# Gating and splitting gelu values inside their PSUM banks, a gates' grid in runs of 16 frames, and one-hot rows by one pointer instruction a frame, in a streaming encoder step

## The chip, the cores and the metric

One core of a Trainium2 chip runs the whole step as one program. The metric is the device time of an execution in microseconds; the kernel before was run three times. TensorE multiplies matrices (its weight loads are shown as a row of their own, PEld), VectorE (DVE) and ScalarE (ACT) work element by element and can read and write PSUM, GpSimd (POOL) works element by element in SBUF and issues the indirect gathers, SyncE (SP) issues the other DMAs. Each engine runs its queue in order.

## The reference

The step is one layer over 1024 prompt frames and 32 sample frames of width 1024: input projection, differential attention, a gated recurrence, output projections, and then PEER, a retrieval over 16384 single-neuron experts. The change touches PEER alone. For each frame, 8 heads each pick 16 experts by the best sums of two key halves; an expert's number is 128 i + j.

```python
s = jnp.einsum('thcd,hckd->thck', q, sub_keys.astype(jnp.float32))
sv, si = lax.top_k(s, P_TOPK)
comb = (sv[:, :, 0, :, None] + sv[:, :, 1, None, :]).reshape(P_TBLOCK, P_HEADS, P_TOPK * P_TOPK)
cv, ci = lax.top_k(comb, P_TOPK)
...
gate = jax.nn.softmax(cv, axis=-1)
hid = jax.nn.gelu(jnp.einsum('thkd,td->thk', down[e], xs).astype(jnp.float32), approximate=False)
return jnp.einsum('thk,thkd->td', (gate * hid).astype(xs.dtype), up[e])
```

The output is the residual sum, normed. Everything is float32; the large products are made of operands split into a rounded high part and a low part, three products for one.

## The kernel before, in words

Frames come in tiles of 128 (0 to 7) and a tile "S" of 32 sample frames. Tiles 0 to 4 ("dense", 640 frames) go through all 16384 experts; tiles 5, 6, 7 and S gather the rows of their own experts. Generators yield pieces of work, each with the time it is taken to cost, and a loop weaves them into one program: `gemm` (the projections, then the dense experts), `attn`, `routing` (the best 16, `topk`), `scatter` (the gates of the dense tiles), `rows` (the gathered experts). `PACED` holds the rows and the routing on VectorE behind what `gemm` has asked of it. A planner then orders each engine's queue by a model of instruction times.

**The gates' grid** (`scatter` and `grid`, L1084 to L1148, 739 to 1604 us). For each dense frame the 128 gates are placed into a 128 x 128 grid by a product of one-hot matrices: rows `am` (is this the expert's i), columns `bm` (is this its j, times the gate). Four frames make a step, 160 steps in all. `bm` is one comparison of 512 elements on VectorE against broadcast operands (L1126) and one multiplication by the gates on GpSimd (L1139). `am` is in every other step one such comparison on VectorE, in the others five ScalarE instructions (L1134, L1135). Four 128 x 128 products go into one bank, and ScalarE copies it (L1091) into the staging tile `stg`. After 16 frames `stg` goes to DRAM, 1 MB, as `W_d`, in which the 8 columns of a group lie side by side for each frame.

**The dense experts** (`hidden` L1156, `stage_v` L1198). A column e stands for the 128 experts 128 i + e. `hidden(e)`: two loads of weights, split by ScalarE and GpSimd (L254, L255, tiles `dh`, `dl`), 24 products into each of two PSUM banks of 320 frames, then ScalarE's gelu from the bank into an SBUF tile `vg` (L1174; the first six columns before `stage_v`, four of them into a tile `early`). `gated(e)`: every 8 columns the gates are loaded from `W_d`, two tiles of 1.25 MB; two VectorE multiplications by the gates, of 320 elements each, whose gates lie 8 elements apart (L1214); then `split`: a rounding copy on ScalarE (L254) and the rest by a subtraction on VectorE (L255), both over 640 elements, into `vwh` and `vwl`. Each four columns are multiplied by the up weights `uh`, `ul`: 8 blocks of two banks of 12 products, each bank added to the sums `acc` in SBUF by VectorE (L1279). All these banks come in turn from one pool of five; a further bank `ws` serves the sum of the sample's runs, and two hold the gathered rows' sums `xp`.

**The gathered rows** (L1044 to L1050, L1031). For each of 416 rows: an indirect gather issued by GpSimd, a product and sum over 1024 elements on VectorE (L1047), gelu and gate on ScalarE, and a multiplication and addition into `xp` in PSUM on VectorE (L1031).

The two lines of the split:

```python
A.activation(h, src, AF.Copy)
(lo_engine or G).tensor_tensor(out=l, in0=src, in1=h.bitcast(F32), op=OP.subtract)
```

Of the kernel before, what the change touches and what calls it, by code (L numbers as in the profile page):

```python
# [7 lines left out]
F32 = mybir.dt.float32  # L8
# [17 lines left out]
JB = 8  # L26

# tiles of frames that share a pass over w_in; tiles that share one over the other weights
AG = [[0, 1, 2, 3, 4], [5, 6, 7, "S"]]
CDG = [[0, 1, 2], [3, 4], [5, 6, 7, "S"]]  # L30
# tiles whose expert products run over all experts; the other ones gather the rows of theirs
# [3 lines left out]
# tiles whose scores wait in DRAM, and how many heads are routed at a time if not all  # L35
DEFER = [6, 7]
HG = {5: 2, 6: 4}
# places of weights in the rings, as they come and in two parts: output stages, then projections
RINGS = [(4, 4), (2, 3), (3, 4), (4, 4)]
SCS = [2, 2, 4, 3]  # L40
# places of the recurrence's tiles, by group
DEEP = [(2, 10), (1, 5)]
# frames on their way into the projections, by group
PRE = [2, 1]
# places of: gathered rows; expert weights, as they come and split; best halves; one-hots
RB, VR, VB, BB, OHB = 4, 3, 2, 4, 4
# engines that make the one-hot rows, in turn
AMS = "DA"
# of the splits of weights in the output stages, one in so many goes to the vector engine
CSH = 2  # L50
# banks of the large products: so many of so many in turn from the extra pool of that size
GX = (3, 6, 3)
# columns of experts whose hidden values wait in the place of the sums
GB, GE = 2, 6
# the time that a gathered row and a one-hot half step are taken to cost
GC, SC = 1.65, 1.0
# which streams keep behind the large products in which phase, and by how much less
# [10 lines left out]
def step_kernel(ctx, tc, x_prompt, x_sample, cache_kT, cache_v, state, norm1, w_in, lam_params,  # L68
# [21 lines left out]
    def bank_of(name):  # L90
        return lambda: P[name].tile([128, 512], F32, name=name, tag=name)
# [4 lines left out]
    gb_bank, gv_bank = bank_of("gb"), bank_of("gv")  # L96
    TURN = [0]

    def gm_bank():
        """ the banks of the large products; more of them while the attention asks for none """  # L100
        TURN[0] += 1
        key = "gx" if "gx" in P and TURN[0] % GX[1] < GX[0] else "gm"
        return P[key].tile([128, 512], F32, name="gm", tag="gm")
# [7 lines left out]
    # ---------------------------------------------------------------- constants  # L111
# [27 lines left out]
    def masks(ct):  # L139
        """ what the attention and the recurrence need of constants """  # L140
        # masks of [s, t]: s <= t inside a block of 16; a block of 16 against the one before it in 32
# [8 lines left out]
        # s - 16*(t//16) in 0..15 and s <= t  # L150
# [5 lines left out]
        # s - 32*(t//32) in 0..15, t in the second half of its 32  # L156
# [4 lines left out]
        # resets of the running sums at each block of 16  # L161
# [9 lines left out]
        # the weight of the second map  # L171
# [10 lines left out]
        # lower bounds of the gates, columns: heads  # L182
# [13 lines left out]
    # ---------------------------------------------------------------- scratch in DRAM  # L196
# [26 lines left out]
    def span(ts):  # L223
        """ runs of consecutive token columns: (first column here, first column in DRAM, width) """
# [10 lines left out]
    def rstd_of(pool, ss, n, width, T=128, tag=""):  # L235
        """ (ss/width + eps)^-0.5 for a [T, n] tile of sums of squares """
        ms = pool.tile([128, n], F32, name="ms" + tag, tag="ms" + tag)
        V.tensor_scalar(ms[:T], ss[:T], 1.0 / width, 1e-6, op0=OP.mult, op1=OP.add)
        # a first guess from the exponent's bits, then Newton's steps
# [17 lines left out]
    def mm3(out, pairs):  # L257
        """ sum of products of operands split into two parts each """
# [6 lines left out]
    def transposed_half(bank, xs, T, hi, lo, off):  # L265
        """ four blocks of 128 columns into a pair of tiles """
# [17 lines left out]
    def load_split(pool, src, tag, rbufs, bufs, nk=KD, share=0):  # L284
        """ a block of weights [128, nk, 256], in two parts, by four blocks of 128 rows """
# [12 lines left out]
    # ---------------------------------------------------------------- input projection  # L298
    BDONE, READY, DONE = set(), set(), set()
    BEST = {}  # L300
    # 0: up to the products over all experts, 1: their start, 2: their steady state
    PHASE = [0]

    def natural(g, b, i, ws, wk):
        """ a block of the projection of one tile, frames by rows """
# [1147 lines left out]
```

## Time and profile before

| | |
|---|---|
| median of 3 runs | 3572.49 us (3570.26 to 3582.99) |
| profiled execution: span | 3583.5 us |
| TensorE, VectorE | 3257.4 us (91%), 3063.6 us (85%) |
| GpSimd, ScalarE | 2074.9 us (58%), 1454.3 us (41%) |

The profile is of one execution. Its own time is given only as the span from the first to the last instruction; that span is 11.0 us above the median of the runs, and no time around it is listed. The busy shares are means over stages with different limits, so the stages are read one by one in the section on rows. Times in the rows are microseconds, "mean ns" is nanoseconds. A name behind "<-" after a bar is what the engine last waited for.

### The profile page before, as it was taken

The numbers are of one execution on the slowest core, as the hardware profiler recorded it, in microseconds if no ns is written. First come the engines' busy times: TensorE is split into PE (matmuls) and PEld (weight loads), VectorE is DVE, ScalarE is ACT, GpSimd is POOL, SyncE is SP. The second block draws the span as 40 slices with busy tenths as digits, with TensorE's granted clock in tenths as the row PEclk, the third lists the DMA queues.
The fourth block names the chain that finished last, engine by engine and source line by source line (L and its number), as shares of the span: only waits on it lengthen the run. The fifth ranks groups of instructions, "written<-read, shape, count | busy, mean of one in ns | idle before, by whom it ended". The sixth has DMA issues, their size and how long they took to land.

```text
span 3583.5 us, 59911 instructions
## 1 busy us (share of the span) xinstructions
PE 3257.4 (91%) x21639; PEld 3128.0 (87%) x21639; DVE 3063.6 (85%) x6101; ACT 1454.3 (41%) x3508; POOL 2074.9 (58%) x1339
## 2 busy tenths in 40 slices
PE   7999899989998887868989988899999999999995
PEld 7989899867877886767889888899999999999994
DVE  3354468999787999999999999988989989989998
ACT  3544334445665544543333323333333333333332
POOL 2322125546444556666666577777767666776674
PEclk9999999999998998978999999999999999999997
DMA  4554364454465644478788777799888998998987
GB/s 164 166 158 149 107 215 158 152 151 152 148 217 183 206 130 150 152 249 298 258 289 296 275 271 290 266 341 351 316 315 335 337 343 296 346 338 333 336 325 265
DMA packets 357304, 880.58 MB, mean 246 GB/s; under 512 B 30960, under 2 KB 190192, under 8 KB 299664
## 3 DMA queue, kind: packets, MB, share of 16 engines
q1 hardware_dynamic: 297104, 440.52, 36.8%
q0 software_dynamic: 59904, 436.23, 33.0%
q8 instruction: 171, 2.80, 0.3%
q14 instruction: 125, 1.02, 0.1%
HBM read 784.47 MB, written 92.14 MB: 245 GB/s over the span
## 4 chain that ended last, share of the span: by engine, by line
PE 28%; DVE 19%; issue 2%; DMA 2%; POOL 2%; ACT 0%; POOLq 0%; ACTq 0%; DVEq 0%
PE gv L263 9%; PE gv L262 9%; PE gv L261 9%; DVE row L1047 5%; DVE xp L1031 5%; DVE vg L1214 2%; DVE acc L1279 2%; DMA ur<-in_p_up_dram 2%; DVE vwl L255 2%; POOL row L1044 1%; DVE oh L967 1%; POOL dl L255 1%; DVE ef L972 1%; POOL ul L255 0%; DVE si L902 0%
## 5 line engine op out<-in xcount | busy, mean ns | idle before, releaser
L1044 POOL DMA_INDIRECT row<-in_p_rows_dram,ei x384 | 559.8, 1458 | 340.2 <-DVE xp L1031 172.2
L255 POOL TENSOR_TENSOR wl<-wr,wh 128x1024 fp32r<-128x1024 f32 x160 | 397.3, 2494 | 532.2 <-ACT wh L254 483.0
L261 PE MATMUL gv<-vxh,dh 128*128 128x320 f32 x2048 | 646.5, 316 | 42.4 <-DVE acc L1279 23.6
L263 PE MATMUL gv<-vxh,dl 128*128 128x320 f32 x2048 | 644.8, 316 | 34.8 <-POOL dl L255 34.7
L261 PE MATMUL gv<-vwh,uh 128*128 128x320 f32 x2048 | 636.2, 311 | 14.1 <-ACT uh L254 8.3
L262 PE MATMUL gv<-vwl,uh 128*128 128x320 f32 x2048 | 636.8, 311 | 12.4 <-DVE vwl L255 12.3
L262 PE MATMUL gv<-vxl,dh 128*128 128x320 f32 x2048 | 642.3, 314 | 0.0
L263 PE MATMUL gv<-vwh,ul 128*128 128x320 f32 x2048 | 633.9, 310 | 1.1 <-POOL ul L255 1.0
L1047 DVE CUSTOM_DVE_ANT_0 row<-row,xg 128x1024 f32<-128x1024 f32 x416 | 627.0, 1507 | 3.1 <-DMA sc<-scs 2.3
L1031 DVE SCALAR_TENSOR_TENSOR xp<-row,hid,xp 128x1024 f32<-128x1024 f32 x412 | 527.8, 1281 | 78.2 <-ACT hid L1050 78.0
L1049 ACT ACTIVATE hid<-hid 128x1 f32<-128x1 f32 x416 | 84.0, 202 | 936.1 <-DVE hid L1047 926.3
L255 POOL TENSOR_TENSOR ul<-ur,uh 128x512 fp32r<-128x512 f32 x256 | 359.7, 1407 | 135.2 <-ACT uh L254 125.6
L261 PEld LDWEIGHTS gv<-vxh,dh 128*128 128x128 f32 x2048 | 393.5, 192 | 50.1 <-DVE acc L1279 27.3
L263 PEld LDWEIGHTS gv<-vxh,dl 128*128 128x128 f32 x2048 | 392.7, 192 | 43.1 <-POOL dl L255 42.0
L255 POOL TENSOR_TENSOR dl<-dr,dh 128x512 fp32r<-128x512 f32 x256 | 365.1, 1433 | 82.0 <-ACT dh L254 73.9
L261 PEld LDWEIGHTS gv<-vwh,uh 128*128 128x128 f32 x2048 | 386.7, 189 | 17.1 <-ACT uh L254 9.3
L262 PEld LDWEIGHTS gv<-vwl,uh 128*128 128x128 f32 x2048 | 386.9, 189 | 16.5 <-DVE vwl L255 16.5
L262 PEld LDWEIGHTS gv<-vxl,dh 128*128 128x128 f32 x2048 | 393.9, 192 | 0.0
L263 PEld LDWEIGHTS gv<-vwh,ul 128*128 128x128 f32 x2048 | 386.3, 189 | 2.7 <-POOL ul L255 2.5
L1139 POOL TENSOR_TENSOR ohB<-ohB,tr 128x512 f32<-128x512 f32 x160 | 195.0, 1224 | 264.3 <-DVE ohB L1126 201.5
L1214 DVE TENSOR_TENSOR vg<-vg,gw 128x320 f32<-128x320 f32 x248 | 253.4, 1022 | 27.7 <-ACT vg L1174 17.5
L261 PE MATMUL gm<-xh,wh 128*128 128x320 f32 (+1 forms) x768 | 254.0, 331 | 0.0
(328 smaller groups left out, 7490.5 us busy)
## 6 DMA issues: line engine op xcount, KB each, us to landing
dr<-in_p_downT_dram SPq DMA_DIRECT2D x256, 256.0 KB
ur<-in_p_up_dram SPq DMA_DIRECT2D x256, 256.0 KB
wr<-in_w_in_dram SPq DMA_DIRECT2D x88, 512.0 KB
W_d<-stg SPq DMA_DIRECT2D x40, 1024.0 KB
gw<-W_d SPq DMA_DIRECT2D x32, 1280.0 KB
wr<-in_p_wq_dram SPq DMA_DIRECT2D x48, 512.0 KB
wr<-in_w_out_dram SPq DMA_DIRECT2D x24, 512.0 KB
wr<-in_w_a_dram SPq DMA_DIRECT2D x12, 512.0 KB
```

What stands on the lines that cost most here:

```text
L255: (lo_engine or G).tensor_tensor(out=l, in0=src, in1=h.bitcast(F32), op=OP.subtract)
L261: PE.matmul(out, lh, rh, start=(i == 0), stop=False)
L262: PE.matmul(out, lh, rl, start=False, stop=False)
L263: PE.matmul(out, ll, rh, start=False, stop=(i == n - 1))
L967: V.tensor_tensor(out=oh[:T], in0=cf[:T, h].unsqueeze(2).to_broadcast([T, 16, NCAND]), in1=iota_c[:T].unsqueeze(1).to_broadcast([T, 16, NC ...
L1031: V.scalar_tensor_tensor(out=acc, in0=row[:, D:], scalar=hid[:, k:k + 1], in1=acc if k else first, op0=OP.mult, op1=OP.add)
L1044: G.indirect_dma_start(out=row, out_offset=None, in_=p_rows, in_offset=bass.IndirectOffsetOnAxis(ap=ei[:, k:k + 1], axis=0))
L1047: V.tensor_tensor_reduce(out=row[:, 0:D], in0=row[:, 0:D], in1=xt, scale=1.0, scalar=0.0, op0=OP.mult, op1=OP.add, accum_out=h)
L1049: A.activation(h, h, AF.Gelu)
L1139: G.tensor_tensor(out=bm, in0=bm, op=OP.mult, in1=tr[:, 2, xs].unsqueeze(2).to_broadcast([128, 4, 128]))
L1214: V.tensor_mul(gh, gh, G_[h][:, :, j])
L1279: V.tensor_add(acc[:, db, cs], acc[:, db, cs], ps[:, :CHUNK])
```

## The change

The gelu of all columns after the first six stays in its PSUM bank. Gating and split work bank by bank, 320 frames at a time, with the bank as operand; the tile `vg` goes away, and the first six columns all use `early`. Every sixth bank asked for once the dense stage has begun is the spare bank `ws`. The grid in DRAM now holds, for each group of 8 columns, runs of 16 frames for one column; the staging copy writes that order. The one-hot rows are made frame by frame, 128 elements at a time, by VectorE comparisons against a number per partition, for `bm` with the gate as a second such number in the same instruction; GpSimd's multiplication goes away. The sample's sum takes its banks from the large pool. Only comments differ elsewhere.

```diff
-GB, GE = 2, 6
...
+GE = 6
...
-    gb_bank, gv_bank = bank_of("gb"), bank_of("gv")
+    gb_bank = bank_of("gb")
     TURN = [0]
 
+    def gv_bank():
+
+        TURN[0] += 1
+        pool, tag = (wsp, "ws") if PHASE[0] and TURN[0] % 6 == 0 else (P["gv"], "gv")
+        return pool.tile([128, 512], F32, name="gv", tag=tag)
...
-                    ps = ws_bank()
+                    ps = gv_bank()
...
-    W_d = dram([128 // JB, 128, NV, JB], "W_d")
     SB = 16
+    W_d = dram([128 // JB, 128, NV // SB, JB, SB], "W_d")
...
-        A.activation(stg[:, :, q:q + 4, :].rearrange("p b t j -> p t b j"),
-                     ps.rearrange("p (t b j) -> p t b j", t=4, j=JB), AF.Copy)
+        A.activation(stg[:, :, :, q:q + 4],
+                     ps.rearrange("p (t b j) -> p b j t", t=4, j=JB), AF.Copy)
         if q + 4 == SB:
-            o = 128 * DENSE.index(t) + s0
-            SP.dma_start(out=W_d[:, :, o:o + SB, :].rearrange("b i t j -> i b t j"), in_=stg)
+            o = (128 * DENSE.index(t) + s0) // SB
+            SP.dma_start(out=W_d[:, :, o].rearrange("b i j t -> i b j t"), in_=stg)
...
-                stg = sct.tile([128, 128 // JB, SB, JB], F32, name="stg", tag="stg", bufs=1)
+                stg = sct.tile([128, 128 // JB, JB, SB], F32, name="stg", tag="stg", bufs=1)
...
-                    xs = slice(s0 + q, s0 + q + 4)
-
-                    def equal(out, row):
-                        V.tensor_tensor(out=out, in0=iota_r.unsqueeze(1).to_broadcast([128, 4, 128]),
-                                        in1=tr[:, row, xs].unsqueeze(2).to_broadcast([128, 4, 128]),
-                                        op=OP.is_equal)
-
+                    for u in range(4):
+                        c = s0 + q + u
+                        if AMS[(s0 + q) // 4 % len(AMS)] == "A":
+
+                            A.activation(am[:, u], iota_r, AF.Abs, bias=tr[:, 3, c:c + 1])
+                        else:
+                            V.tensor_scalar(am[:, u], iota_r, tr[:, 0, c:c + 1], None, op0=OP.is_equal)
+                        V.tensor_scalar(bm[:, u], iota_r, tr[:, 1, c:c + 1], tr[:, 2, c:c + 1],
+                                        op0=OP.is_equal, op1=OP.mult)
                     if AMS[(s0 + q) // 4 % len(AMS)] == "A":
...
-                        for u in range(4):
-                            c = s0 + q + u
-                            A.activation(am[:, u], iota_r, AF.Abs, bias=tr[:, 3, c:c + 1])
                         A.activation(am, am, AF.Relu, bias=1.0, scale=-1.0)
-                    else:
-                        equal(am, 0)
-                    equal(bm, 1)
-                    G.tensor_tensor(out=bm, in0=bm, op=OP.mult,
-                                    in1=tr[:, 2, xs].unsqueeze(2).to_broadcast([128, 4, 128]))
...
-        if GB <= e < GE:
-            g = VX["early"][:, e - GB]
-        else:
-            g = wk.tile([128, NV], F32, name="vg", tag="vg", bufs=GB)
+        VX[e] = []
         for cs in CS:
             ps = gv_bank()
             mm3(ps[:, :CHUNK], [(dn[k], (VX["xh"][:, k, cs], VX["xl"][:, k, cs])) for k in range(KD)])
-            A.activation(g[:, cs], ps[:, :CHUNK], AF.Gelu)
-        VX[e] = g
+
+            g = VX["early"][:, e, cs] if e < GE else ps[:, :CHUNK]
+            A.activation(g, ps[:, :CHUNK], AF.Gelu)
+            VX[e].append(g)
...
-                        G_[h] = P["gw"].tile([128, n // 2, JB], F32, name="gw", tag="gw", bufs=2)
-                        SP.dma_start(out=G_[h], in_=W_d[b, :, h * (n // 2):(h + 1) * (n // 2), :])
-                g = VX[e]
-                for h in range(2):
-                    gh = g[:, h * (n // 2):(h + 1) * (n // 2)]
-                    V.tensor_mul(gh, gh, G_[h][:, :, j])
+                        m = n // 2 // SB
+                        G_[h] = P["gw"].tile([128, m, JB, SB], F32, name="gw", tag="gw", bufs=2)
+                        SP.dma_start(out=G_[h], in_=W_d[b, :, h * m:(h + 1) * m])
                 wh = wk.tile([128, n], F32R, name="vwh", tag="vwh", bufs=WR)
                 wl = wk.tile([128, n], F32R, name="vwl", tag="vwl", bufs=WR)
-                split(wh, wl, g, V)
+                for cs, g, gates in zip(CS, VX[e], G_.values()):
+                    gt = g.rearrange("p (m s) -> p m s", s=SB)
+                    V.tensor_tensor(out=gt, in0=gt, in1=gates[:, :, j], op=OP.mult)
+                    split(wh[:, cs], wl[:, cs], g, V)
                 ws[e] = (wh, wl)
```

## Rows read from the trace of the kernel before

**Rows 1.** Stages: start:end, length, busy us (instructions) per engine, clock, DMA share, GB/s.
```profile
core 0: us, PE busy (x) PEld busy (x) DVE busy (x) ACT busy (x) POOL busy (x), PEclk, DMA share, GB/s
739.00:1200.00 461.00, 413.59 (x2825) 361.02 (x2824) 397.29 (x892) 261.28 (x650) 240.02 (x141) 0.94 0.57 176
1200.00:1604.00 404.00, 319.49 (x1991) 301.34 (x1992) 385.60 (x1024) 201.18 (x453) 235.91 (x147) 0.89 0.52 168
1604.00:2340.00 736.00, 651.67 (x4162) 634.05 (x4161) 721.55 (x1338) 240.38 (x612) 504.79 (x334) 0.95 0.78 283
2340.00:3500.00 1160.00, 1151.73 (x7821) 1146.52 (x7820) 1059.89 (x1369) 416.47 (x1085) 819.46 (x582) 1.00 0.90 332
```
**Rows 2.** TensorE's waits, 1604 to 2340 us: us in total, times, longest.
```profile
PE gv L261 <- DVE acc L1279: 28.4, 18, 5.3
PE gv L263 <- POOL dl L255: 26.3, 17, 6.0
...
PE gv L262 <- DVE vwl L255: 10.5, 11, 1.9
```
**Rows 3.** Groups by line, 1604 to 2340 us: count, busy us, mean ns, idle before.
```profile
L1214 DVE TENSOR_TENSOR vg<-vg,gw 128x320 f32<-128x320 f32 x82 | 90.4, 1104 | 0.0
L1279 DVE TENSOR_TENSOR acc<-acc,gv 128x320 f32<-128x320 f32 x151 | 70.0, 471 | 0.0
L255 DVE TENSOR_TENSOR vwl<-vg,vwh 128x640 fp32r<-128x640 f32 x42 | 59.5, 1420 | 0.4 <-ACT vwh L254 0.4
...
L1044 POOL DMA_INDIRECT row<-in_p_rows_dram,ei x134 | 194.4, 1450 | 145.3 <-DVE xp L1031 45.2 <-DVE ci L904 14.8 <-DVE tmpc L901 13.4
```
**Rows 4.** Single lines, whole run: count, ns at least, in the middle and at most.
```profile
L1214 DVE TENSOR_TENSOR vg<-vg,gw x248: 702/805/2767, 1586.0 to 3496.6; 128x320 f32<-128x320 f32 x124
...
L255 DVE TENSOR_TENSOR vwl<-vg,vwh x124: 795/830/4243, 1640.9 to 3505.3; 128x640 fp32r<-128x640 f32 x124
...
L1279 DVE TENSOR_TENSOR acc<-acc,gv x496: 423/476/514, 1716.4 to 3549.5; 128x320 f32<-128x320 f32 x166
...
L1031 DVE SCALAR_TENSOR_TENSOR xp<-row,hid,xp x412: 1224/1280/1312, 1555.8 to 3570.4; 128x1024 f32<-128x1024 f32 x138
```
**Rows 5.** 2340 to 3500 us: ScalarE's gelu (group), and VectorE's wait for it.
```profile
L1174 ACT ACTIVATE vg<-gv 128x320 f32<-128x320 f32 x164 | 69.3, 423 | 49.5 <-PE gv L263 46.4 <-DVE vwl L255 2.7 <-issue 0.3
...
DVE vg L1214 <- ACT vg L1174: 17.5, 17, 3.7
```
**Rows 6.** Groups of the one-hot rows, 739 to 1604 us, and the spread of L1126.
```profile
L1126 DVE TENSOR_TENSOR ohB<-iota_r,tr 128x512 f32<-128x512 f32 x160 | 154.0, 966 | 5.7 <-PE ws L1090 5.7
L1126 DVE TENSOR_TENSOR ohA<-iota_r,tr 128x512 f32<-128x512 f32 x80 | 70.3, 879 | 8.1 <-PE ws L1090 7.9
...
L1139 POOL TENSOR_TENSOR ohB<-ohB,tr 128x512 f32<-128x512 f32 x160 | 195.0, 1224 | 264.3 <-DVE ohB L1126 201.5 <-DVE mx L478 10.9 <-PE gm L263 8.0
...
L1091 ACT ACTIVATE stg<-ws 128x512 f32<-128x512 f32 x160 | 92.7, 593 | 91.9 <-DMA W_d<-stg 50.1 <-PE ws L1090 41.4
...
L1126 DVE TENSOR_TENSOR ohB<-iota_r,tr x160: 659/682/2895, 744.4 to 1590.7; 128x512 f32<-128x512 f32 x160
```
**Rows 7.** VectorE in order of time (start us, us), then L948's group and spread.
```profile
127.90 0.61 DVE L408 TENSOR_SCALAR zt<-zt,oml,lb 128x640 f32<-128x640 f32 x1 [0.98 <-ACT zt L395]
130.90 0.49 DVE L412 TENSOR_SCALAR zt<-zt 128x640 f32<-128x640 f32 x1 [2.39 <-ACT zl L411]
...
711.00 0.99 DVE L967 TENSOR_TENSOR oh<-cf,iota_c 128x800 f32<-128x800 f32 x1
711.91 0.49 DVE L408 TENSOR_SCALAR zt<-zt,oml,lb 128x416 f32<-128x416 f32 x1
...
L948 DVE TENSOR_SCALAR sf<-sf 128x128 f32<-128x128 f32 x6 | 2.9, 480 | 0.0
...
L948 DVE TENSOR_SCALAR sf<-sf x13: 161/209/1897, 658.7 to 2018.9; 128x128 f32<-128x128 f32 x6, 128x32 f32<-128x32 f32 x4, 128x64 f32<-128x64 f32 x2, 32x128 f32<-32x128 f32 x1
```
**Rows 8.** TensorE's waits, 1200 to 1604 us: us in total, times, longest.
```profile
PE ws L1090 <- POOL ohB L1139: 19.5, 11, 6.0
```

## The prediction

> **What bounds the kernel now.** I read the stages first: busy time of each engine in five stretches [rows 1]. From 2340 to 3500 us TensorE works 1151.7 of 1160 us at a granted clock of 1.00. A saving on VectorE buys nearly nothing there. From 1604 to 2340 it is the other way round: VectorE 721.6 of 736 us, TensorE 651.7 at a clock of 0.95. From 1200 to 1604 VectorE works 385.6 of 404; from 739 to 1200 it has 64 us free. So VectorE limits two stretches, and the change touches its load in both: the gating and the split in the later one, the one-hot rows in the earlier.
>
> Next, what TensorE waits for from 1604 to 2340 [rows 2]: 28.4 us for VectorE's additions to the sums, 10.5 for the low half of the split, 26.3 for GpSimd's `dl`. Then who fills VectorE there [rows 3]: the gating (82 at 1.104 us) and the split's subtraction (42 at 1.420) hold 149.9 us. The addition L1279, with as many elements as one gating, costs 0.471.
>
> The spread of single instructions tells why [rows 4]. The gating takes 0.702 at least, 0.805 in the middle, 2.767 at most; the subtraction 0.795, 0.830 and 4.243. Both read two operands from SBUF. L1279, with one operand in PSUM, stays between 0.423 and 0.514, and L1031, which also writes PSUM, between 1.224 and 1.312. So two things inflate the gating: waits, which instructions with one PSUM operand do not show, and its gates lying 8 elements apart, since its 320 elements take almost as long as the subtraction's 640.
>
> **The gating and the split.** A column had two gatings and one subtraction of 640: 2 x 1.104 + 1.420 = 3.63 us. It will have two gatings and two subtractions, each of 320 elements, one operand in PSUM and one in SBUF in runs of 16 or more. The bounds are L1279's 0.471 and, for the gating, its own 0.805 if the stride's cost stayed. I take 0.471: L1031 shows that writing PSUM adds nothing, since its 1.28 for 1024 elements is less per element. In the stretch 166 x 0.471 = 78 replace 149.9, 72 us less; at 98% fill the stretch could lose 73. TensorE would allow more: its 4162 products at the later stretch's pace (1160/7821 = 0.148 us) need 617 us, 119 less than 736. Its stalls on VectorE and on `dl`, which queues behind gathers that wait for VectorE [rows 2, 3], sum to 65 us. I take 65; the ends are 39 (VectorE's own two) and 73.
>
> ScalarE's rounding copy of 640 becomes two of 320, at most 2 x 0.423 a column by L1174, beside an engine with two thirds of its time free [rows 1, 5]. The gelu writes its bank instead of SBUF, for which I take the same 0.423. The handovers from gelu to gating and from copy to subtraction exist already: VectorE waited 17.5 us for the first in the last long stretch [rows 5] and 0.4 for the second in the one before [rows 3]. Twice that fits into the 100 us that VectorE has free in the long stretch; behind such a wait stand the gathered rows' instructions, which have slack there. The early six columns stay in SBUF: under 5 us either way, counted as nothing.
>
> A hidden bank is now held until the subtraction ends. A column takes two hidden banks and four for the up products, and every sixth turn uses the spare bank, so a bank is asked for again one column later. In the long stretch a column is 1160/7821 x 96 = 14.2 us. Filling takes 3.6 (24 products), which leaves 10.6 for gelu, gating, copy and subtraction, some 1.9 of work. I cost it at nothing; what covers it is that VectorE's queue is less than about 8 us late. Of the 8.3 us that TensorE stands idle in that stretch I let 5 go.
>
> **The one-hot rows.** Removed are 160 + 80 comparisons on VectorE (224.3 us) and 160 products on GpSimd (195.0 us) [rows 6]. Added are 640 comparisons with two pointers and 320 with one, each 128 wide. The trace has no such row. The nearest [rows 7]: 640 wide, 0.61 us with two pointers and 0.49 without, so 0.06 a pointer; 416 wide with two, 0.49. By that slope 128 wide with two is 0.335, with one 0.275; without pointers L948's middle is 0.209. Neighbours overlap by 0.08 (a start at 711.91 before an end at 711.99), so the turns are 0.255 and 0.195, and 640 x 0.255 + 320 x 0.195 = 226 us, against 206 now counted the same way. Of the 206, 240 x (0.682 - 0.08) = 144 is work and 61 waiting. GpSimd keeps 281 of its 476 busy us [rows 1, 6]; waits in proportion to its load and to the burst length are 61 x 226/144 x 281/476 = 57. So 283 against 206: 77 more. The rest of VectorE's 783 us waits less: if a tenth of those 577 is waiting, 41% of it is 23; between 0 and that I take 15. Net 62, half of it before 1200, where 64 free us hide it. After 1200 there are 31 on an engine with 18 free: 25 come through. The 19.5 us that TensorE waits for GpSimd's product [rows 8] go, half of them into the next wait: -10. Together 15 longer; the ends are 43 shorter and 82 longer (the rivals below).
>
> [...]
>
> ScalarE's copy into the staging tile now reads PSUM at a stride and writes runs of 4: between its 0.593 [rows 6] and, if a stride costs what it costs the gating (about 1 ns an element), 1.1. That is up to 80 us on an engine with 53% load there; I count nothing. The grid's stores and loads keep their number, size and runs in DRAM, nothing moves on SyncE's queue, and GpSimd's queue only loses the products.
>
> **Sum.** -65 - 5 + 15 = -55. The profiled span is 3583.5, so the new one 3528.5; the old one lies 11.0 above the median 3572.49, and with the same offset the median becomes 3518. Its own range, 39 to 73 won and 35 to 0 lost on the one-hots: 3494 to 3563. A measurement of this kernel tells about 0.5%, 18 us, from no change.
>
> **The rivals.**
> Cheap comparisons: pointers cost nothing in a burst and one takes 0.209. Then 960 x 0.129 = 124 plus 31 of waits is 51 less than now, 66 with the relief; half of it, and the 10 of TensorE, make the early stretch 43 shorter, and the later one wins 75: 3450. For it: short independent neighbours overlap. Against: the price of pointers in rows 7.
> The stride stays: in-place gating at 0.805 saves 3.63 - 2 x 0.805 - 2 x 0.471 = 1.08 a column, 44 for 41 columns; -44 - 5 + 15 gives 3538. The change would not do what it says. Against: runs of 16.
> GpSimd becomes the bound: `dl` still comes late behind gathers of 1.45 us [rows 3], only 39 is won and the one-hots cost 35: 3563.
> Slower, the comparisons wait for GpSimd: L948 averages 0.480 over its six 128-wide instructions and reaches 1.897 [rows 7], so a one-source instruction does wait. At 0.48 the 960 take 384 us, 163 more net; 75 come through after 1200 and 17 before, and 92 - 10 - 70 leaves 12 longer, 3584. From 0.49 on it is above 3590, at 0.55 it is 3651. Against: 41% of GpSimd's work there is gone. [...]
> Late banks: if a hidden bank comes back 1 us too late in each of 82 columns of the long stretch, 82 us are lost, 3604. Against: 10.6 us of room. For: the banks' return now hangs on the fullest queue.
>
> **Chances.** Forecast 0.48 (0.43 of it below 3554), cheap comparisons 0.22, stride 0.07, GpSimd 0.11, waits of comparisons 0.08, late banks 0.04. So faster 0.43 + 0.22 + 0.07 = 0.72, the same 0.05 + 0.11 = 0.16, slower 0.08 + 0.04 = 0.12. The range runs from the cheap case, 3450, to the edge of the slower ones, 3590; it leaves out those 0.12 and the lower tail of the cheap case.
>
> **What would show it.** Right: gating and both subtractions near 0.47 with maxima under 0.6; the long full stretch of TensorE ending some 55 us sooner; no product on GpSimd; 960 comparisons near 0.3 with tails over 1 us. Wrong: a mean near 0.49 there, new stalls of TensorE that name the gelu's bank, or a long stretch above 14.2 us a column.

## The result, and the profile after

The changed kernel takes 3708.65 us (median of 4 runs, 3704.73 to 3711.03) against 3575.56 for the kernel before (4 runs). The ratio is 1.0372, 95% interval 1.0351 to 1.0394: 133 us slower, where 55 less had been forecast. The profiled span is 3703.0 us. All ratios below are against runs of the kernel before on the same chip, and a difference between two runs is the difference of their ratios, times some 3577 us for the kernel before.

The page of the changed kernel, the span and the busy time of each engine:

```profile
span 3703.0 us, 60611 instructions
...
PE 3261.3 (88%) x21639; PEld 3133.3 (85%) x21639; DVE 2927.8 (79%) x6949; ACT 1487.5 (40%) x3634; POOL 1810.1 (49%) x1179
```

VectorE is busy 136 us less than the 3063.6 of before and GpSimd 265 less; TensorE does the same work in a longer span. The stages (columns as in [rows 1]):

```profile
739.00:1200.00 461.00, 411.03 (x2766) 359.15 (x2766) 413.63 (x1212) 259.35 (x650) 130.08 (x59) 0.94 0.54 169
1200.00:1604.00 404.00, 324.96 (x2045) 307.20 (x2045) 382.28 (x1374) 200.75 (x434) 120.32 (x60) 0.89 0.49 162
1604.00:2340.00 736.00, 657.82 (x4229) 645.09 (x4229) 700.81 (x1467) 262.35 (x700) 508.49 (x356) 0.94 0.83 305
2340.00:3500.00 1160.00, 1003.24 (x6750) 992.36 (x6749) 934.76 (x1391) 398.20 (x1093) 741.21 (x540) 0.94 0.87 324
```

Up to 2340 us little differs from before: from 1604 on TensorE does 4229 products where it did 4162. The loss is in the long stretch, 6750 against 7821. TensorE's waits there, 2340 to 3703 us (us in total, times, longest):

```profile
PE gv L1074 <- DVE fnb L1071: 137.7, 1, 137.7
PE gv L267 <- DVE acc L1277: 15.2, 16, 5.1
```

One wait of 137.7 us. It is the product that sums the sample's four runs (L1074), waiting for the copy of the sample's sums (L1071). The timeline of TensorE around it:

```profile
2745.34 0.31 PE L269 MATMUL gv<-vwh,ul 128*128 128x320 f32 x1
2883.35 3.62 PE L1074 MATMUL gv<-fnb,runs 128*32 128x512 f32 x4 [137.70 <-DVE fnb L1071]
```

And what VectorE does in those us (groups by line, 2746 to 2882 us):

```profile
L1037 DVE SCALAR_TENSOR_TENSOR xp<-row,hid,xp 128x1024 f32<-128x1024 f32 x41 | 52.8, 1287 | 17.9 <-ACT hid L1056 17.3
L1053 DVE CUSTOM_DVE_ANT_0 row<-row,xg 128x1024 f32<-128x1024 f32 x42 | 51.2, 1220 | 10.0 <-DMA row<-in_p_rows_dram,es 7.8 <-DMA xg<-xn_S 2.0
...
L1277 DVE TENSOR_TENSOR acc<-acc,gv 128x320 f32<-128x320 f32 x1 | 0.5, 487 | 0.4 <-PE gv L269 0.4
```

42 gathered rows and one addition of the products: VectorE works through the rows, busy for 106 of these 136 us, until the sample's last is done. By the code, the sum's turn in the ring (the large pool, whose banks are handed out in order) fixes its place among the products in TensorE's queue, and whatever stands behind it there waits with it; e1 and e3 test this. In the kernel before the sum had a bank of its own, and TensorE waited 0.3 us for it.

The single lines of the change, whole run (count: ns at least/middle/most, first and last start us):

```profile
L1214 DVE TENSOR_TENSOR gv<-gv,gw x244: 468/494/500, 1673.7 to 3644.5; 128x320 f32<-128x320 f32 x122
...
L261 DVE TENSOR_TENSOR vwl<-gv,vwh x244: 459/481/494, 1700.5 to 3652.7; 128x320 fp32r<-128x320 f32 x122
...
L1136 DVE TENSOR_SCALAR ohB<-iota_r,tr x640: 316/334/2552, 744.4 to 1569.1; 128x128 f32<-128x128 f32 x160
...
L1135 DVE TENSOR_SCALAR ohA<-iota_r,tr x320: 256/274/2450, 744.2 to 1566.9; 128x128 f32<-128x128 f32 x160
...
L1097 ACT ACTIVATE stg<-ws x160: 570/597/625, 748.0 to 1576.2; 128x512 f32<-128x512 f32 x160
...
L1277 DVE TENSOR_TENSOR acc<-acc,gv x496: 445/479/489, 1711.0 to 3682.3; 128x320 f32<-128x320 f32 x166
...
L1037 DVE SCALAR_TENSOR_TENSOR xp<-row,hid,xp x412: 1256/1287/1292, 1596.9 to 3461.7; 128x1024 f32<-128x1024 f32 x138
```

Gating and subtraction are as short and as even as forecast. The last two lines matter for all that follows: two strands run to the end of the program, the products (their last addition starts at 3682.3) and the gathered rows (3461.7). Before, they ended at 3549.5 and 3570.4 [rows 4]: **the rows ended last**, by 21 us. After, the products do, by 220.

### The profile page after: what moved, and what is told of

The parts are those of the page before. It is cut to its first block, busy times and chain, and to the rows that moved or that the text cites. A ratio compares the mean times of both kernels' runs of the same rounds, so it can differ in the third digit from the quotient of the medians.

```text
span 3703.0 us, 60611 instructions
## 1 busy us (share of the span) xinstructions
PE 3261.3 (88%) x21639; PEld 3133.3 (85%) x21639; DVE 2927.8 (79%) x6949; ACT 1487.5 (40%) x3634; POOL 1810.1 (49%) x1179
## 4 chain that ended last, share of the span: by engine, by line
PE 59%; DVE 26%; DMA 7%; issue 4%; ACT 2%; POOL 2%; SPq 0%; DVEq 0%; ACTq 0%; POOLq 0%
PE gv L267 12%; PE gv L269 12%; PE gv L268 12%; PE gm L267 6%; PE gm L268 6%; PE gm L269 6%; DVE row L1053 4%; DVE xp L1037 4%; DVE ohB L1136 4%; PE ws L1096 2%; DMA row<-in_p_rows_dram,ei 2%; DVE ohA L1135 1%; DVE oh L973 1%; DVE acc L1277 1%; PE gb L474 1%
## 5 line engine op out<-in xcount | busy, mean ns | idle before, releaser
L261 POOL TENSOR_TENSOR wl<-wr,wh 128x1024 fp32r<-128x1024 f32 x160 | 388.0, 2438 | 866.2 <-ACT wh L260 739.3
L267 PE MATMUL gv<-vwh,uh 128*128 128x320 f32 x2048 | 645.3, 315 | 71.8 <-DVE acc L1277 58.6
L269 PE MATMUL gv<-vxh,dl 128*128 128x320 f32 x2048 | 636.9, 312 | 7.2 <-POOL dl L261 7.2
L1050 POOL DMA_INDIRECT row<-in_p_rows_dram,ei x384 | 495.9, 1291 | 286.6 <-DVE xp L1037 159.9
L1053 DVE CUSTOM_DVE_ANT_0 row<-row,xg 128x1024 f32<-128x1024 f32 x416 | 601.1, 1445 | 24.0 <-DMA row<-in_p_rows_dram,ei 13.9
L261 POOL TENSOR_TENSOR ul<-ur,uh 128x512 fp32r<-128x512 f32 x256 | 371.0, 1449 | 203.5 <-ACT uh L260 188.8
L1277 DVE TENSOR_TENSOR acc<-acc,gv 128x320 f32<-128x320 f32 x496 | 235.1, 479 | 102.4 <-PE gv L269 97.2
L260 ACT ACTIVATE uh<-ur 128x512 fp32r<-128x512 f32 x256 | 161.4, 631 | 294.5 <-PE gv L268 170.8
L1136 DVE TENSOR_SCALAR ohB<-iota_r,tr 128x128 f32<-128x128 f32 x640 | 263.9, 443 | 15.2 <-PE ws L1096 15.0
```

What stands on the lines that cost most here:

```text
L267: PE.matmul(out, lh, rh, start=(i == 0), stop=False)
L269: PE.matmul(out, ll, rh, start=False, stop=(i == n - 1))
L1050: G.indirect_dma_start(out=row, out_offset=None, in_=p_rows, in_offset=bass.IndirectOffsetOnAxis(ap=ei[:, k:k + 1], axis=0))
L1053: V.tensor_tensor_reduce(out=row[:, 0:D], in0=row[:, 0:D], in1=xt, scale=1.0, scalar=0.0, op0=OP.mult, op1=OP.add, accum_out=h)
L1136: V.tensor_scalar(bm[:, u], iota_r, tr[:, 1, c:c + 1], tr[:, 2, c:c + 1], op0=OP.is_equal, op1=OP.mult)
L1277: V.tensor_add(acc[:, db, cs], acc[:, db, cs], ps[:, :CHUNK])
```

## The experiments

### Is it the sum's bank, the held banks, or the comparisons?

**e1.** The changed kernel, the sum put into the two banks of `xp`, whose contents have just been copied out.

```diff
-                    ps = gv_bank()
+                    ps = acc[:, c * 512:(c + 1) * 512]
```

> The changed kernel, with only the sample's sum taken out of the ring of the large products: it goes into the two banks of xp that have just been copied out. Theory 1 (the sum's bank, asked for in the ring, makes the products behind it wait for all of the sample's rows, 137.7 us at one place): the stall of 137.7 us at the sum's product is gone, and the time is near 3709 - 138 = 3571, from 3555 to 3585. Theory 2 (hidden banks held until the split come back late): the sum is only where the lateness shows; the time stays above 3670. Theory 3 (the one-hot comparisons, 155 us more on VectorE, put the rows behind): the same, above 3670.

3572.65 us, ratio 0.9975 (0.9963 to 0.9988). The stall is gone and with it 0.0397 of 3576, 142 us. Theory 1 holds. The ends of its two strands:

```profile
L1277 DVE TENSOR_TENSOR acc<-acc,gv x496: 451/480/489, 1709.1 to 3546.0; 128x320 f32<-128x320 f32 x166
...
L1037 DVE SCALAR_TENSOR_TENSOR xp<-row,hid,xp x412: 1256/1287/1292, 1597.7 to 3498.4; 128x1024 f32<-128x1024 f32 x138
```

The rows end 72 us earlier than before, the products 3.5. What gating and split give back went almost wholly into the strand that is now not the last.

**e2.** The changed kernel with the sum in the spare bank again and five banks in the ring.

```diff
-        pool, tag = (wsp, "ws") if PHASE[0] and TURN[0] % 6 == 0 else (P["gv"], "gv")
-        return pool.tile([128, 512], F32, name="gv", tag=tag)
+        return P["gv"].tile([128, 512], F32, name="gv", tag="gv")
...
-                    ps = gv_bank()
+                    ps = ws_bank()
```

> The changed kernel with the banks as they were before: the sum in the spare bank, five banks in the ring, no turn with the spare one. Theory 1: the stall at the sum goes here too, near 3571, and one bank less in the ring costs or saves under 20 us. Theory 2: with one bank less the hidden banks are scarcer still; at least as slow as the changed kernel, above 3700. Theory 4 (the sixth turn itself couples the ring with the sum): this one is faster than the sum in xp by more than 20 us.

3651.43, ratio 1.0193 (1.0173 to 1.0212). The stall is gone here too, but one bank less costs 78 us against e1, not under 20: TensorE's waits for the additions are 71.1 us from 1604 to 2340 (53.6 in e1) and 39.5 from 2340 to 3500 (18.2). So banks are scarce in this kernel; theory 2 was wrong on the stall and right that the held banks cost something.

**e3.** The kernel before, with the sum alone moved into the ring.

```diff
-                    ps = ws_bank()
+                    ps = gv_bank()
```

> The kernel before, with one line changed: the sample's sum asks the ring of the large products for its two banks. Theory 1: a stall of TensorE of about 120 to 150 us at the sum's first product, and a time near 3575 + 135 = 3710 (3680 to 3730). Theories 2 and 3: nothing else of the change is in it, so it stays at 3575 within 20.

3716.72, ratio 1.0376 (1.0349 to 1.0403): this one line reproduces the loss of the whole change. TensorE's waits, 2340 to 3720 us:

```profile
PE gv L1068 <- DVE fnb L1065: 167.6, 1, 167.6
```

The products' last addition starts at 3699.2, 150 us later than before. The span grows by 136 and not by 150, mainly since the rows had ended 21 us after the products.

**e4.** The kernel before, with the one-hot rows of the change alone.

```diff
-                        equal(am, 0)
-                    equal(bm, 1)
-                    G.tensor_tensor(out=bm, in0=bm, op=OP.mult,
...
+                            V.tensor_scalar(am[:, u], iota_r, tr[:, 0, c:c + 1], None, op0=OP.is_equal)
+                        V.tensor_scalar(bm[:, u], iota_r, tr[:, 1, c:c + 1], tr[:, 2, c:c + 1],
+                                        op0=OP.is_equal, op1=OP.mult)
```

> The kernel before, with only the one-hot rows of the change. Theory 3: slower by 50 to 155 us, 3625 to 3730, the stretch until 1604 longer by that. Theory 1: the comparisons take VectorE some 150 us more, but what they displace has slack until the dense stage; 3575 within 25, either side. The forecast's term was 15 longer.

3606.36, ratio 1.0066 (1.0047 to 1.0084): 24 us slower, at the edge of theory 1's 25 and short of theory 3's 50. The first rows' addition, in this kernel:

```profile
L1031 DVE SCALAR_TENSOR_TENSOR xp<-row,hid,first x3: 1265/1294/1382, 1589.9 to 3017.2; 128x1024 f32<-128x1024 f32 x3
```

In the kernel before that line reads 1551.1. The rows start 39 us later and end 27 later (3597.1), as the last strand. So the comparisons seem to cost time through the rows' start, and not through the scatter's end: the staging copy's last start is 1603.8 before and 1585.6 here.

### Where did the gating's 65 us go?

**e5.** As e1, with the old one-hot rows.

```diff
-                    for u in range(4):
-                        c = s0 + q + u
...
+                    equal(bm, 1)
+                    G.tensor_tensor(out=bm, in0=bm, op=OP.mult,
+                                    in1=tr[:, 2, xs].unsqueeze(2).to_broadcast([128, 4, 128]))
```

> The changed kernel with the sum in xp and the old one-hot rows (one comparison of 512 for bm, GpSimd's product). If the pointer comparisons cost here what they cost alone (3606 against 3579, 27 us), the time is 3573 - 27 = 3546, from 3535 to 3558, and the stretch until the scatter's last copy is shorter. If that price belonged to the old order alone (the gating and split hide it), it stays at 3573 within 10.

3562.14, ratio 0.9941 (0.9919 to 0.9963); against e1 the pointers cost 0.0034, 12 us, and both expectations miss by a little. Its products end at 3539.3 and its rows at 3478.7.

**e6.** As e5, the rows' model cost `GC` by tile.

```diff
-GC, SC = 1.65, 1.0
+GC, SC = 1.65, 1.0
+GCT = {5: 1.9}
...
-                yield GC
+                yield GCT.get(t, 1.55)
```

> As the run before it, with the gathered rows of tile 5 taken to cost 1.9 instead of 1.65 a half row and those of the later tiles 1.55, so that some 18 of the 153 rows that fell between 1604 and 2340 us come later. Theory 5 (the VectorE time that gating and split gave up went to rows that ran earlier, 43 us for 16 rows, so TensorE still waits there for the additions, 54 us): 20 to 45 us faster than the run before it, near 3515. Rival (the long stretch, with the DMA engines at 0.91 and VectorE at 83%, has no room for the rows): the same within 10 us or slower.

3556.18, ratio 0.9934 (0.9917 to 0.9950), not to be told from e5. The lever did not act: 151 rows from 1604 to 2340 where e5 has 152. It decides nothing; e11 pulls harder.

**e7.** The kernel before with six banks and the sum in `xp`: `gv_bank` of the change, and the edit of e1.

> The kernel before with the ring of six banks (every sixth turn the spare bank) and the sample's sum in xp, its gelu still into SBUF. The changed kernel lost 79 us when it went from six banks to five. If a bank more is worth something by itself, this is faster than 3579 by 30 us or more, and TensorE's waits for the additions fall from 28 us between 1604 and 2340. If the sixth bank only makes up for the banks that gelu, gating and split hold, this is the same within 15 us.

3573.90, ratio 0.9993 (0.9978 to 1.0008). The same: the sixth bank is worth no time where no gelu value is held in one. It did act, from 1604 to 2340: the waits for the additions fell from 28.4 to 5.7 us, but those for `dl` rose from 26.3 to 42.4 and those for `vwl` from 10.5 to 18.0.

**e8.** The kernel before with the gates' grid in runs of 16 alone; gelu and gating stay in SBUF, the sum in the spare bank.

```diff
-                        G_[h] = P["gw"].tile([128, n // 2, JB], F32, name="gw", tag="gw", bufs=2)
...
-                    gh = g[:, h * (n // 2):(h + 1) * (n // 2)]
+                        m = n // 2 // SB
+                        G_[h] = P["gw"].tile([128, m, JB, SB], F32, name="gw", tag="gw", bufs=2)
...
+                    gh = g[:, h * (n // 2):(h + 1) * (n // 2)].rearrange("p (m s) -> p m s", s=SB)
```

> The kernel before with only the gates' grid in runs of 16 frames: the gating still multiplies SBUF by SBUF. If the stride of 8 was what made a gating take 0.805 in the middle, its minimum falls from 0.702 to 0.40 to 0.47 and 82 of them give back some 27 us between 1604 and 2340; the time is 3550 to 3570. [...]

3553.37, ratio 0.9919 (0.9902 to 0.9936): 29 us from a layout, half of what the fastest run (e13) wins. Its gating:

```profile
L1215 DVE TENSOR_TENSOR vg<-vg,gw x248: 459/486/3376, 1582.0 to 3466.7; 128x320 f32<-128x320 f32 x124
```

The minimum falls from 0.702 to 0.459 us [rows 4], the maximum does not (3.376). So the stride made the work, and the waits stayed with the two SBUF operands (3.376 us here, 0.492 at most in e10, where one of the two lies in PSUM), as the prediction had read the two from one row.

**e9.** As e5, the gelu into an SBUF tile `vg` of two places instead of its bank; halves of 320 and six banks stay.

```diff
-            g = VX["early"][:, e, cs] if e < GE else ps[:, :CHUNK]
+            g = (VX["early"][:, e] if e < GE else vg)[:, cs]
```

> As e5 (sum in xp, old one-hot rows, grid in runs of 16, six banks), but the gelu writes SBUF again, so that gating and split, still in halves of 320, have no bank to hold. Theory 6 (the hidden banks held through gelu, gating, copy and subtraction make TensorE wait for the bank after them: 50 us of waits for the additions between 1604 and 2340, 19.5 after, against 18 and 0 with the grid alone): those waits fall under 25 and 5 us and the time is 3545 to 3556, under e5 by 6 to 17 us, although gating and subtraction cost VectorE more. Rival (what counts is VectorE's time, some 60 us less of it with operands in PSUM): slower than e5 by 10 us or more.

3565.63, ratio 0.9965 (0.9953 to 0.9977). The waits behaved as theory 6 says (for the additions 6.3 us and none, after 50.4 and 19.5), and VectorE as the rival says (1604 to 2340 us):

```profile
L261 DVE TENSOR_TENSOR vwl<-vg,vwh 128x320 fp32r<-128x320 f32 x80 | 77.3, 982 | 0.1
...
L1222 DVE TENSOR_TENSOR vg<-vg,gw 128x320 f32<-128x320 f32 x82 | 61.1, 745 | 0.0
```

TensorE waits 57 us there for `dl` and `vwl` where e5 waits 8. The two nearly cancel: 9 us above e5, with intervals that overlap.

**e10.** As e5, but the gating reads the bank and writes SBUF; the split follows there, over 640.

```diff
+                vg = P["va"].tile([128, n], F32, name="vg", tag="vg", bufs=2)
...
-                    V.tensor_tensor(out=gt, in0=gt, in1=gates[:, :, j], op=OP.mult)
-                    split(wh[:, cs], wl[:, cs], g, V)
+                    V.tensor_tensor(out=vt, in0=gt, in1=gates[:, :, j], op=OP.mult)
+                split(wh, wl, vg, V)
```

> As e5, but the gating reads gelu's bank and writes SBUF, and the split works on 640 elements there: the bank comes free after the gating. Theory 6: waits for the additions between those of e9 and e5, gating at 0.47 to 0.49, subtraction back at 0.8 to 1.4 for 640; time 3540 to 3556. Rival: as e5, 3562 within 6, if holding a bank up to the gating is as bad as up to the subtraction.

3539.03, ratio 0.9885 (0.9868 to 0.9901), faster than e5 by 20 us. Waits for the additions: 3.6 us and none. With one operand in PSUM the gating stayed even, whether it wrote SBUF, as here (0.492 us at most), or PSUM, as in the changed kernel (0.500):

```profile
L1222 DVE TENSOR_TENSOR vg<-gv,gw x244: 458/483/492, 1665.9 to 3455.1; 128x320 f32<-128x320 f32 x122
```

**e11, e12.** As e5 and as e10, with tile 5's rows at 2.45 in the diff of e6.

> As e5, with the rows of tile 5 paced at 2.45: 26 rows fewer (137 instead of 163) stand ahead of the 160th addition in VectorE's queue; the 1.9 of e6 had put off two. Theory 5 (rows take the time that the change frees): the waits for the additions between 1604 and 2340 fall by half, 25 us or more, and the time to 3525 to 3545. Rival (rows are not what the additions wait for, or the long stretch pays it back): within 8 us of e5, 3562.

> As e10, with the rows of tile 5 paced at 2.45 as in e11: both reasons at once. Theories 5 and 6 together: the fastest of all, 3515 to 3540. If either gives nothing, within 6 us of e10 or of e11.

e11: 3583.25, ratio 1.0016 (1.0006 to 1.0025). e12: 3568.22, ratio 0.9967 (0.9955 to 0.9978). Both slower than what they are made from, and theory 5 falls. This time the lever acted: 128 rows from 1604 to 2340 instead of 152, and VectorE stood idle, as its groups in e11 there show:

```profile
L1285 DVE TENSOR_TENSOR acc<-acc,gv 128x320 f32<-128x320 f32 x160 | 75.3, 475 | 41.7 <-PE gv L270 41.5
L1222 DVE TENSOR_TENSOR gv<-gv,gw 128x320 f32<-128x320 f32 x85 | 41.4, 488 | 28.7 <-ACT gv L1180 27.2 <-ACT dh L261 1.3
```

Yet TensorE still waits 45.2 us for the additions (50.4 in e5): they do not wait for the rows. And the late rows end last, at 3571.8 and 3564.0, behind products that end at 3534.1 and 3494.0.

### What holds the banks?

In the changed kernel itself, ScalarE's gelus and its copies into `vwh` (timeline, 2387 to 2413 us):

```profile
2387.10 0.42 ACT L1172 ACTIVATE gv<-gv 128x320 f32<-128x320 f32 x1 [2.99 <-PE gv L269]
...
2391.06 0.42 ACT L1172 ACTIVATE gv<-gv 128x320 f32<-128x320 f32 x1
...
2401.18 0.42 ACT L1172 ACTIVATE gv<-gv 128x320 f32<-128x320 f32 x1 [1.33 <-PE gv L269]
...
2405.14 0.42 ACT L1172 ACTIVATE gv<-gv 128x320 f32<-128x320 f32 x1
...
2411.26 1.10 ACT L260 ACTIVATE vwh<-gv 128x320 fp32r<-128x320 f32 x3 [0.76 <-PE gv L269]
```

Four gelus, the third and fourth column of a block, and no copy until 2411.26, when TensorE (the releaser) has ended the block before. A bank that was ready at 2387.5 is held 24 us. The code says why: `vwh` and `vwl` have six places (`WR`), and the four columns of a block are all read until its last product, so two places are left for four new columns. Before, the values waited for the same places, but in SBUF.

Worked out from the single instructions, from each gelu's end to the start of its copy, 2340 to 3500 us, in the middle: 1.1 and 0.9 us for the first two columns of a block, 23.6 for the third, 10.3 for the fourth. The prediction had 10.6 us of room.

**e13.** As e5, one place more.

```diff
-    JU, WR = 4, 6
+    JU, WR = 4, 7
```

> As e5 (gating and split inside the banks), with seven places for the split columns vwh and vwl instead of six; nothing else. Theory 7 (a block of four columns keeps four of the six places until its last product, so the third and fourth column of the next block can't be split and keep their four banks until then): one of the two late columns is freed; the waits for the additions fall from 50 to under 35 us between 1604 and 2340 and from 19.5 to under 10 after, and the time to 3542 to 3556. Rival (the banks wait for the subtraction's turn in VectorE's queue behind rows): 3562 within 6 and the waits as they were.

3523.07, ratio 0.9842 (0.9818 to 0.9866): 35 us less than e5, more than expected, and 56 less than the kernel before, the fastest of all. TensorE's waits for the additions, 1604 to 2340 us, in e5 and then here:

```profile
PE gv L267 <- DVE acc L1284: 50.4, 18, 9.4
...
PE gv L267 <- DVE acc L1284: 12.6, 3, 5.2
```

From 2340 to 3500 the products' 19.5 us of them are gone, and the third column's hold falls from 22.5 to 0.8 us, the fourth's from 10.3 to 6.2. Its strands:

```profile
L1284 DVE TENSOR_TENSOR acc<-acc,gv x496: 450/477/489, 1695.6 to 3472.8; 128x320 f32<-128x320 f32 x166
...
L1037 DVE SCALAR_TENSOR_TENSOR xp<-row,hid,xp x412: 1257/1284/1292, 1565.2 to 3510.9; 128x1024 f32<-128x1024 f32 x138
```

Both strands are some 60 to 77 us earlier than before. Against e5 the products end 67 us earlier, but the rows 32 later.

**e14, e16.** Eight places, with two places of `ur` instead of three for the room; and two places of `ur` alone.

```diff
-    JU, WR = 4, 6
+    JU, WR = 4, 8
...
-                        ur = wk.tile([128, JU, 128], F32, name="ur", tag="ur", bufs=VR)
+                        ur = wk.tile([128, JU, 128], F32, name="ur", tag="ur", bufs=2)
```

> As e5, with eight places for vwh and vwl, so that no column waits for one; to find the room, the weights ur have two places instead of three. Theory 7: waits for the additions under 15 and 3 us, the long stretch of TensorE full again (7800 products or more), time 3528 to 3548, if the place of ur costs nothing. Rival: 3562 or slower, waits for the additions as they were.

> As e5, with two places of ur instead of three: what the room that e14 takes costs by itself. 3562 within 6 if two loads ahead are enough; if the weights come late, TensorE waits for uh and it is 10 us or more slower.

e14: 3533.08, ratio 0.9865 (0.9839 to 0.9891); e16: 3549.66, ratio 0.9914 (0.9892 to 0.9935), not slower than e5. The places alone give 0.0049, 18 us. The waits for the additions are as expected (8.2 and 2.4 us), and the middle hold of each column is 0.8 to 1.8 us in the long stretch. But that stretch has 7724 products, not 7800, and e14 is not faster than e13: waits for `vwl` (25.6 us against 14.5 in e13, 1604 to 2340) and for `uh` (once 11.8 against 7.7, later) are longer. Whether `ur`'s two places make the second stays open; e16, which has them too, has no such wait after 2340.

**e15.** As e10, with the pointer one-hot rows.

> As e10 (3539), with the pointer one-hot rows of the change. If they cost what they cost in the change (e1 against e5, 10 us) or in the kernel before (27 us): 3549 to 3566. If the gating's saving hides them: 3539 within 6.

3560.97, ratio 0.9949 (0.9929 to 0.9970): 23 us for the pointers, as in the kernel before.

**e17.** As e1, with the edit of e13: the change with both couplings undone.

> The changed kernel with its two couplings undone and nothing else: the sum in xp, and seven places for vwh and vwl; its pointer one-hot rows stay. e13 is the same with the old one-hot rows, 3523. By theory 7 and the price of the pointers (10 to 22 us): 3533 to 3545, and waits for the additions under 20 us between 1604 and 2340. If the places only helped together with the old one-hots, it stays near e1, 3573.

3569.31, ratio 0.9970 (0.9953 to 0.9987), a miss: 46 us over e13, and only 2 below e1. So the seventh place, worth 35 us with the old one-hot rows, is worth nothing clear of noise with the pointers, as the last sentence of the expectation allowed. It acts all the same: the waits are near what was expected (23.5 us), the third column's hold is 0.9 us, and the products end 43 us before e1's. But:

```profile
L1277 DVE TENSOR_TENSOR acc<-acc,gv x496: 455/477/489, 1706.6 to 3503.0; 128x320 f32<-128x320 f32 x166
...
L1037 DVE SCALAR_TENSOR_TENSOR xp<-row,hid,xp x412: 1256/1284/1298, 1593.8 to 3557.5; 128x1024 f32<-128x1024 f32 x138
```

The rows set the end now, at 3557.5, 47 us after e13's; their first addition starts at 1592.3 against 1561.9, which is 30 of the 47. Against e1 they end 59 us later, though they start no later (1596.2 there). In e5 and e13 too the rows lost while the products won. Both strands run on VectorE; how its time is shared between them wasn't tried.

**e18.** The kernel before with seven places, and two of `ur` for the room.

> The kernel before with seven places for vwh and vwl, and two of ur for the room. There the gelu waits for its place in SBUF and holds no bank, so by theory 7 the seventh place frees nothing: 3579 within 15 us, TensorE's waits for dl and for vwl between 1604 and 2340 as before, 26 and 10 us. Rival (a further place of the split columns is worth some 39 us to any of these kernels): 3530 to 3555.

3608.87, ratio 1.0070 (1.0046 to 1.0095). The seventh place brings no 35 us here, though it acts: from 2340 on the third column waits in SBUF for 4.0 us in the middle, where it waited 20.1. But this kernel has `ur`'s two places as well, so it does not show by itself what the seventh place is worth. That e13's 35 us come from the banks rests on e10, which frees the banks with six places and wins 20, and on the holds and waits of e13 and e14. That this kernel is 25 us slower was in neither expectation. Its waits for `dl` and for the additions are 5.8 and 5.4 us longer from 1604 to 2340, and those for `ul`, which is split from `ur`, are 8.4 us where there were none, and 9.4 against 1.0 after. That points at `ur`, whose two places cost e16 nothing; the cause stays open.

## Why the prediction was wrong

**The step that failed** is one that the prediction does not have. The text ahead of it says "The sample's sum takes its banks from the large pool", and the prediction gives this moved step no cost and no line, though it goes through the queues of VectorE, GpSimd and SyncE. It should have asked what stands behind the sum in the ring and how late the sum's input is. e1 and e3 give it 142 and 135 us, more than all other terms together, and 3709 lies outside the range of 3450 to 3590.

**"A hidden bank is now held until the subtraction ends … I cost it at nothing"** failed too. The prediction set 1.9 us of work against 10.6 of room and left out that the copy needs a place in `vwh`. The hold is 24 us in the place shown and 23.6 in the middle for every third column. Undoing it is worth 35 us (e5 to e13) or 20 (e5 to e10) with the old one-hot rows, but only 2 (e1 to e17) or 9 (e1 to e15) with the pointers, where the rows then end last. The rival of the late banks had the right place, but feared VectorE's queue; e11 shows that it is not that.

**Gating and subtraction at 0.471** came out at 0.484 and 0.476 on average, with the waits gone [rows 3]: right in size (changed kernel, 1604 to 2340 us).

```profile
L1214 DVE TENSOR_TENSOR gv<-gv,gw 128x320 f32<-128x320 f32 x82 | 39.7, 484 | 8.5 <-ACT gv L1172 5.8 <-DMA gw<-W_d 2.6
...
L261 DVE TENSOR_TENSOR vwl<-gv,vwh 128x320 fp32r<-128x320 f32 x80 | 37.0, 476 | 4.2 <-ACT vwh L260 4.2
...
PE gv L267 <- DVE acc L1277: 50.2, 19, 7.7
```

They take 77 us where 149.9 stood. That this makes the stretch 65 shorter was wrong: TensorE does 67 products more, 10 us at the pace of the prediction. Waits for `dl` fell from 26.3 to 5.1 us as forecast, but those for the additions rose from 28.4 to 50.2, for the held banks, and VectorE's time went to 18 more gathered rows.

The waits are as the prediction read them from [rows 4]: the gating's maxima are 0.500 (the changed kernel) and 0.492 us (e10) with one operand in PSUM, 3.376 with two in SBUF (e8). What GpSimd does beside them fits: in the kernel before 62 of the 248 gatings take 1.000 us or more, and all 62 run beside a GpSimd operation on two tensors, against 26 of the 186 shorter ones; in the changed kernel 81 of 244 run beside one, and none takes more than 0.500.

**The rule on what ends last.** "A saving on VectorE buys nearly nothing there" read the long stretch by TensorE's share alone. The rows' last addition at 3570.4, after the products' 3549.5, stood in [rows 4] and was not read. Two strands that end nearly together mean that a gain counts only where both get shorter: against the kernel before, e1 shortens mainly the rows, e12 and e17 mainly the products, and e8, e10, e13 and e14 both.

**The one-hot rows.** The prices 0.335 and 0.275, worked out from the slope of wider rows, were 0.334 and 0.274 in the middle. With waits an instruction takes 0.443 and 0.360 on average. Counted as the forecast counts, each less 0.08, all take 322 us, more than the 283 forecast. The 15 us longer are 24 in e4, 12 between e5 and e1, 23 between e10 and e15 and 46 between e13 and e17. Where the rows end last (e4, e15, e17) they go with a later start of the rows, by 39, 38 and 30 us, and not with "half of it before 1200, where 64 free us hide it"; that the later start is their cause is inferred.

**ScalarE's copy into the staging tile** at nothing: right, 0.597 us in the middle, by either read order (the changed kernel and the kernel before).

**The sum** of -55 against 3573 is near what e13 reaches, -56; but e13 lacks the pointers, which the forecast counts as 15 longer: without them it says -70. With them (e17) the change without its couplings gives 0.0030, 11 us.

**The other rivals.** Cheap comparisons fell with the prices above. The stride did not stay: the gating in its bank takes 0.468 at least. GpSimd did not become the bound, with 5.1 us of waits for `dl`. The rival that came out slower by the comparisons has the right sign for them, but its price, 75 + 17 - 10 = 82 us, is well above the 12 to 46 measured, since it took 0.48 for each; and it put most of it into the stretch after 1200 and not into the rows' start. Why the rows start later wasn't tried.

## What to carry to other kernels

Before a tile is moved into a shared ring of banks, ask how late its producer is and what stands behind it: a ring hands its banks out in order, and one late user stopped all for 137.7 us here. Before a value is left in a bank, follow it to the place that it needs next, and count that place's free copies, not the work on the way. And where several strands run to the end of a program, read the last start of each before pricing a gain on one.

## What the runs showed of the hardware

A gating of 320 elements whose second operand lies 8 elements apart takes 0.702 us at least, in runs of 16 0.459 (e8): about 0.76 ns an element for the stride. ScalarE's staging copy, reading PSUM in another order, took the same 0.597 in the middle as in the kernel before. The sample's sum, products of 512 columns, took 1.061 us each right after TensorE's 138 us of standing, at a granted clock of 0.50 (2883 to 2887 us; 0.51 while it stood), and 0.605 in the kernel before at 1.00 (2993 to 2999 us), where TensorE had been busy for 112.4 of the 113.4 us ahead; e1 has the same 0.605. A subtraction of two SBUF operands cut into halves of 320 costs 0.982 us a half where the whole of 640 cost 1.420 (e9 and [rows 3], 1604 to 2340 us). That the waits come more per instruction than per element is what this suggests; the two kernels differ in their banks too.
